# Where the lo half of a split weight begins in its buffer, in a one-core encoder kernel

## The chip, the core and the metric

The kernel runs on one core of a Trainium2 chip. The metric is the device time of one execution in microseconds; the time of before is the median of three executions.

## The reference, cut to what matters

A two-layer encoder over 256 tokens of width 1024, in float32. Each layer is a chain of matrix products with four mixers in between:

```python
for i in range(DEPTH):                     # 2
    h = rmsnorm(x, norm1_g[i])
    z = h @ w_in[i]
    ...
    gt = jax.nn.sigmoid(gates.reshape(B, S, N_BRANCH, D_MODEL))
    m = (gt[:, :, 0] * (ya @ proj_a[i]) + gt[:, :, 1] * (yb @ proj_b[i])
         + gt[:, :, 2] * (yc @ proj_c[i]) + gt[:, :, 3] * (yd @ proj_d[i]))
    x = x + m @ w_out[i]
    h2 = rmsnorm(x, norm2_g[i])
    x = x + jnp.square(jax.nn.relu(h2 @ mlp_w1[i])) @ mlp_w2[i]
```

## The kernel before, in words

**Splitting.** A float32 product is made of three matmuls of a shorter format (float32r). Each operand is split into a hi part (a rounded copy) and a lo part (what the rounding lost). `mm3` (L246) issues hi by hi, hi by lo and lo by hi, on the lines L248, L249 and L250, all adding to one accumulator.

**Weights.** The weights come from memory in units of up to 1 MB, in the fixed order of `layer_order` (L90). SP issues their DMAs ahead into three raw buffers (`load_raw`, L205). `split_to` (L217) cuts a unit into two halves and makes two tiles of each: ScalarE copies the raw half into the hi tile (L230), VectorE subtracts hi from raw into the lo tile (L231). There are five hi buffers and five lo buffers of 1152 columns; a half has up to 1024 columns, or 1152 in one unit. `take` (L236) hands the halves out in order and keeps up to four split ahead.

**Where a half begins.** `part_offsets` (L85) gives the column at which the hi and the lo half begin in their buffers. Units in MOVING begin at column 112 (448 bytes) in both, all others at column 0. In the program's layout every hi and lo buffer starts 128 bytes past a multiple of 512, every activation tile (pools `s4` and `s2`) 64 bytes past one, and the constant `gm` 192 bytes past one. So a half of a MOVING unit begins 64 past a multiple of 512, as the activations do, and any other half 128 past. Slices of 128 columns are 512 bytes, so all slices of a half have the residue of its start.

**Two ways of use.** `chunk_tm` (L252) and the down projection of the MLP load the activations into the array (128 tokens) and stream the weights over them, 288 to 512 columns at a time: these are the MOVING units, in the profile `w<-hi,act`, `w<-lo,act` and `acc<-...`. `unit_fm` (L285) does the reverse: 128 columns of the weights are loaded into the array, and the activations of 256 tokens stream. In the profile these are `w<-act,hi` and `w<-act,lo` (what streams stands first, then what is loaded): the gates (16 units a layer), the four output projections (8), the MLP's up projection (14 of its 16 units) and the query, key and convolution inputs (8).

In `unit_fm` all k steps of a block run back to back, three matmuls each:

```python
for k in range(nk):
    self.mm3(p[:, b % 2, :], wh[:, k, c], wl[:, k, c], ah[:, k, :], al[:, k, :], k == 0, k == nk - 1)
```

So L248 loads hi and streams the activations' hi part, L249 loads the same hi slice again and streams their lo part, and L250 loads the lo slice and streams the hi part. A triple is one k step. The chip loads the weights of a matmul while the one ahead of it streams (PEld in the profile).

Other work that the prediction names: L695 multiplies the constant `gm` with a split operand `g`; the dilated mixer's units use `chunk_tm` with a stride of 2, so that every second token is loaded.

Of the kernel before, what the change touches and what calls it, by code (L numbers as in the profile page):

```python
# [81 lines left out]
MOVING = {u for u, (mat, k0, nk, cols, off, n) in PLAN.items() if n // nk > 256 and not u.startswith("proj")}  # L82


def part_offsets(l, u):  # L85

    return (112, 112) if u in MOVING else (0, 0)


def layer_order():  # L90
# [38 lines left out]
class Kern:  # L129
# [87 lines left out]
    def split_to(self, upto):  # L217
        nc = self.nc
        while self.hi_ < min(upto, len(self.halves)):
            i, j = self.halves[self.hi_]  # L220
            self.load_raw(i + 1)
            hs = halves(self.units[i][1])
            (k0, k1), (c0, c1) = hs[j]
            src = self.raw[i][:, k0:k1, c0:c1]
            if j == len(hs) - 1:
                del self.raw[i]
            nk, w = k1 - k0, c1 - c0
            hi, lo = [self.hp.tile([128, 1152], F32, tag=t, name=self.nm(t))[:, o:o + nk * w].rearrange(
                "p (k c) -> p k c", k=nk) for t, o in zip(("hi", "lo"), part_offsets(*self.units[i]))]
            nc.scalar.copy(hi.bitcast(F32R), src)  # L230
            nc.vector.tensor_sub(lo.bitcast(F32R), src, hi)  # L231
            self.ready[self.hi_] = (hi.bitcast(F32R), lo.bitcast(F32R))
            self.hi_ += 1
            self.load_raw(i + NRAW)
# [1090 lines left out]
```

## Time and profile before

| | |
|---|---|
| median of 3 executions | 1109.08 us (1108.99 to 1109.64) |
| the profiled execution | 1108.95 us |
| its span, first to last instruction | 1107.1 us |
| granted TensorE clock over the span | 1.000 |
| PE busy | 1089.1 us, 98% |
| weight loads (PEld) busy | 979.8 us, 89% |
| VectorE busy | 729.4 us, 66% |
| ScalarE busy | 581.8 us, 53% |
| moved by DMA | 195.84 MB, mean 177 GB/s |

The span is the time from the program's first to its last instruction in the one profiled execution; what lies around it makes the rest of that execution's time. Matmuls are pipelined: a matmul's reported duration overlaps the next one's, so the distance between two starts tells what a matmul costs in a stream, and the duration tells it only in comparison with others of the same form.

### The profile page before, as it was taken

What the parts mean: (1) busy time and instruction counts of PE and PEld (TensorE: products, weight loads), DVE (VectorE), ACT (ScalarE), POOL (GpSimd) and SP (SyncE); (2) the same over time, 40 slices, a digit from 0 to 9 for tenths busy, and PEclk for the clock granted to TensorE, in tenths of its full rate; (3) what the DMA queues carried; (4) which work ended last, traced back from release to release, by engine and by line L of the source; (5) the groups of instructions that cost most, each with busy time, mean ns of one, the idle gap of its engine ahead of it and who ended that gap; (6) DMA issues with size and microseconds to landing.
All of it is one profiled execution on the core that took longest, in us unless ns stands there. A gap on an engine that the chain in (4) does not pass through costs nothing.

```text
span 1107.1 us, 17951 instructions
## 1 busy us (share of the span) xinstructions
PE 1089.1 (98%) x7374; PEld 979.8 (89%) x7374; DVE 729.4 (66%) x1053; ACT 581.8 (53%) x902; POOL 65.3 (6%) x72
## 2 busy tenths in 40 slices
PE   7999999999999999999999999999999999999998
PEld 4889778999999789889879997889999998999997
DVE  5787777656766668655565777776587667555554
ACT  6765555555544565454547554555464456544442
POOL 1001132000100000000000013130001000000000
PEclk9999999999999999999999999999999999999999
DMA  8443544755354555545445434548443655454542
GB/s 306 167 154 123 188 166 152 213 168 191 115 218 163 199 204 188 190 154 227 155 150 210 156 135 185 185 138 213 164 163 136 226 191 186 156 214 167 209 172 77
DMA packets 41527, 195.84 MB, mean 177 GB/s; under 512 B 5025, under 2 KB 16194, under 8 KB 20196
## 3 DMA queue, kind: packets, MB, share of 16 engines
q1 hardware_dynamic: 41444, 194.68, 49.7%
q8 instruction: 58, 0.95, 0.3%
q14 instruction: 25, 0.20, 0.0%
HBM read 193.58 MB, written 1.08 MB: 176 GB/s over the span
## 4 chain that ended last, share of the span: by engine, by line
PE 91%; DVE 4%; POOL 2%; issue 1%; ACT 1%; DMA 0%; SPq 0%; DVEq 0%; POOLq 0%; ACTq 0%
PE w L248 22%; PE w L250 22%; PE w L249 22%; PE acc L248 5%; PE acc L249 5%; PE acc L250 5%; PE tp L317 3%; DVE lo L231 2%; POOL s L310 2%; PE p L824 1%; PE p L854 1%; PE p L1028 1%; PE p L948 1%; PE p L913 1%; PE w L614 1%
## 5 line engine op out<-in xcount | busy, mean ns | idle before, releaser
L231 DVE TENSOR_TENSOR lo<-raw,hi 128x1024 fp32r<-128x1024 f32 (+2 forms) x352 | 414.5, 1198 | 136.8 <-ACT hi L230 132.9
L248 PE MATMUL w<-act,hi 128*128 128x256 f32 x1440 | 409.6, 284 | 0.0
L250 PE MATMUL w<-act,lo 128*128 128x256 f32 x1440 | 402.7, 280 | 0.0
L249 PE MATMUL w<-act,hi 128*128 128x256 f32 x1440 | 402.7, 280 | 0.0
L230 ACT CAST hi<-raw 128x1024 fp32r<-128x1024 f32 (+2 forms) x352 | 348.9, 1031 | 27.6 <-ACT hi L230 13.0
L248 PEld LDWEIGHTS w<-act,hi 128*128 128x128 f32 x1440 | 271.9, 189 | 8.9 <-issue 3.7
L249 PEld LDWEIGHTS w<-act,hi 128*128 128x128 f32 x1440 | 272.4, 189 | 2.0 <-issue 0.7
L250 PEld LDWEIGHTS w<-act,lo 128*128 128x128 f32 x1440 | 271.0, 188 | 0.0
L248 PE MATMUL w<-hi,act 128*128 128x512 f32 (+1 forms) x416 | 164.9, 396 | 1.6 <-ACT act L404 1.3
L250 PE MATMUL w<-hi,act 128*128 128x512 f32 (+1 forms) x416 | 160.2, 385 | 1.4 <-DVE act L325 1.4
L249 PE MATMUL w<-lo,act 128*128 128x512 f32 (+1 forms) x416 | 160.0, 385 | 1.4 <-DVE lo L231 1.4
L248 PEld LDWEIGHTS w<-hi,act 128*128 128x128 f32 x416 | 79.2, 190 | 17.7 <-issue 1.7
L250 PEld LDWEIGHTS w<-hi,act 128*128 128x128 f32 x416 | 79.1, 190 | 17.7 <-DVE act L325 2.3
L249 PEld LDWEIGHTS w<-lo,act 128*128 128x128 f32 x416 | 79.2, 191 | 16.8 <-DVE lo L231 2.3
L248 PE MATMUL acc<-hi,u 128*128 128x512 f32 x224 | 87.6, 391 | 0.0
L249 PE MATMUL acc<-lo,u 128*128 128x512 f32 x224 | 87.4, 390 | 0.0
L250 PE MATMUL acc<-hi,u 128*128 128x512 f32 x224 | 87.1, 389 | 0.0
L1109 ACT ACTIVATE u<-w 128x512 f32<-128x512 f32 x28 | 16.7, 598 | 115.6 <-PE w L250 115.6
L1111 DVE TENSOR_TENSOR u<-u 128x512 f32<-128x512 f32 x28 | 19.4, 692 | 87.6 <-ACT u L1109 87.5
L1060 ACT ACTIVATE sg<-w 128x512 f32<-128x512 f32 x32 | 19.1, 597 | 86.9 <-PE w L250 86.9
L310 POOL TENSOR_TENSOR s<-s,mhalf 128x8 f32<-128x8 f32 (+2 forms) x32 | 55.2, 1726 | 2.7
L250 PEld LDWEIGHTS acc<-hi,u 128*128 128x128 f32 x224 | 42.1, 188 | 9.0
(231 smaller groups left out, 977.7 us busy)
## 6 DMA issues: line engine op xcount, KB each, us to landing
raw<-in_w SPq DMA_DIRECT2D x166, 1024.0 KB, 4.9
raw<-in_w SPq DMA_DIRECT2D x8, 512.0 KB, 3.3
raw<-in_w SPq DMA_DIRECT2D x4, 576.0 KB, 4.3
b<-bias SPq DMA_DIRECT2D x32, 64.0 KB, 6.7
b<-bias SPq DMA_DIRECT2D x16, 128.0 KB, 6.8
b<-bias SPq DMA_DIRECT2D x8, 256.0 KB, 5.3
w<-in_hw SPq DMA_DIRECT2D x2, 512.0 KB, 6.5
decay<-in_decay SPq DMA_DIRECT2D x2, 512.0 KB, 7.1
```

The costliest lines, as they stand in the source:

```text
L230: nc.scalar.copy(hi.bitcast(F32R), src)
L231: nc.vector.tensor_sub(lo.bitcast(F32R), src, hi)
L248: mm(out, lhsT=lh, rhs=rh, start=start, stop=False)
L249: mm(out, lhsT=lh, rhs=rl, start=False, stop=False)
L250: mm(out, lhsT=ll, rhs=rh, start=False, stop=stop)
L310: self.nc.gpsimd.tensor_tensor(y, x, self.mhalf[:, 0:n], ALU.pow)
L317: self.nc.tensor.transpose(p[:, i, :], s, self.ident)
L614: nc.tensor.matmul(ps[e], lhsT=fw[:, e, ri], rhs=src[:, e], start=True, stop=True)
L824: nc.tensor.matmul(ps[par][:, c0:c0 + k.stop - k.start], lhsT=st.q[g][r, hp, c], rhs=kk, start=True, stop=True)
L1060: self.unit_fm(f"gate_{b}.{2 * i + j}", act, lambda _, ps: nc.scalar.activation(sg[:, 2 * j:2 * j + 2], ps, AF.Tanh, scale=0.5))
L1109: nc.scalar.activation(r, ps, AF.Relu)
L1111: nc.vector.tensor_mul(sq, r, r)
```

## The change

In units that are not in MOVING the lo half begins at column 32 of its buffer, 128 bytes further on than before. The hi half stays at column 0.

```diff
 def part_offsets(l, u):
 
-    return (112, 112) if u in MOVING else (0, 0)
+    return (112, 112) if u in MOVING else (0, 32)
```

The loaded lo slices thus begin 256 bytes past a multiple of 512, where the hi slices begin 128 past and the streamed activations 64 past one. No instruction is added or taken away.

## Rows read from the trace of the kernel before

**Rows 1.** The page, parts 1 and 2: busy time and share; granted clock in 40 slices.

```profile
PE 1089.1 (98%) x7374; PEld 979.8 (89%) x7374; DVE 729.4 (66%) x1053; ACT 581.8 (53%) x902; POOL 65.3 (6%) x72
...
PEclk9999999999999999999999999999999999999999
```

**Rows 2.** The page, part 4: chain that ended last, shares of the span by engine.

```profile
PE 91%; DVE 4%; POOL 2%; issue 1%; ACT 1%; DMA 0%; SPq 0%; DVEq 0%; POOLq 0%; ACTq 0%
```

**Rows 3.** The page, part 5: groups by line and operation, whole run (busy us, mean ns).

```profile
L248 PE MATMUL w<-act,hi 128*128 128x256 f32 x1440 | 409.6, 284 | 0.0
L250 PE MATMUL w<-act,lo 128*128 128x256 f32 x1440 | 402.7, 280 | 0.0
L249 PE MATMUL w<-act,hi 128*128 128x256 f32 x1440 | 402.7, 280 | 0.0
L248 PEld LDWEIGHTS w<-act,hi 128*128 128x128 f32 x1440 | 271.9, 189 | 8.9 <-issue 3.7
L249 PEld LDWEIGHTS w<-act,hi 128*128 128x128 f32 x1440 | 272.4, 189 | 2.0 <-issue 0.7
L250 PEld LDWEIGHTS w<-act,lo 128*128 128x128 f32 x1440 | 271.0, 188 | 0.0
```

**Rows 4.** Groups by form in the stretch 103.5 to 108.6 us.

```profile
L249 PE MATMUL w<-act,hi 128*128 128x256 f32 x16 | 4.4, 276 | 0.0
...
L249 PEld LDWEIGHTS w<-act,hi 128*128 128x128 f32 x16 | 3.0, 188 | 0.0
```

**Rows 5.** Groups by form in the stretch 857.5 to 862.8 us.

```profile
L249 PE MATMUL w<-act,hi 128*128 128x256 f32 x16 | 4.5, 281 | 0.0
...
L250 PEld LDWEIGHTS w<-act,lo 128*128 128x128 f32 x16 | 3.0, 188 | 0.0
...
L248 PEld LDWEIGHTS w<-act,hi 128*128 128x128 f32 x15 | 2.9, 192 | 0.0
```

**Rows 6.** Timeline of PE, 103.4 to 108.9 us: start us, us; first and last.

```profile
103.36 0.28 PE L248 MATMUL w<-act,hi 128*128 128x256 f32 x1
...
108.69 0.28 PE L250 MATMUL w<-act,lo 128*128 128x256 f32 x1
```

**Rows 7.** Timeline of PE, 857.4 to 863.1 us: first and last.

```profile
857.37 0.28 PE L248 MATMUL w<-act,hi 128*128 128x256 f32 x1
...
863.02 0.28 PE L248 MATMUL w<-act,hi 128*128 128x256 f32 x1
```

**Rows 8.** Groups by form from 915 us to the end.

```profile
L249 PEld LDWEIGHTS w<-act,hi 128*128 128x128 f32 x224 | 42.9, 192 | 0.5
```

**Rows 9.** Groups by form in the stretch 253.6 to 258.9 us.

```profile
L250 PEld LDWEIGHTS w<-act,lo 128*128 128x128 f32 x15 | 2.9, 192 | 0.0
```

**Rows 10.** The page, part 5: the down projection's matmuls and loads.

```profile
L248 PE MATMUL acc<-hi,u 128*128 128x512 f32 x224 | 87.6, 391 | 0.0
...
L250 PEld LDWEIGHTS acc<-hi,u 128*128 128x128 f32 x224 | 42.1, 188 | 9.0
```

**Rows 11.** Groups by form, 114.4 to 119.4 us: activations loaded with every second column.

```profile
L249 PE MATMUL w<-lo,act 128*128 128x512 f32 x8 | 3.2, 396 | 0.0
...
L249 PEld LDWEIGHTS w<-lo,act 128*128 128x128 f32 x7 | 1.4, 196 | 0.3
```

**Rows 12.** Timeline of PE, 63.7 to 64.45 us.

```profile
63.83 0.64 PE L695 MATMUL p<-gm,g 128*128 128x256 f32 x4
64.31 0.28 PE L248 MATMUL w<-act,hi 128*128 128x256 f32 x1
```

**Rows 13.** VectorE's splits (rows 11's stretch, rows 5's), busy share, PE's waits on it.

```profile
L231 DVE TENSOR_TENSOR lo<-raw,hi 128x1024 fp32r<-128x1024 f32 x4 | 4.7, 1218 | 0.0
...
L231 DVE TENSOR_TENSOR lo<-raw,hi 128x1024 fp32r<-128x1024 f32 x1 | 1.2, 1227 | 0.3 <-ACT hi L230 0.3
...
PE w L249 <- DVE lo L231: 1.4, 2, 1.0
```

## The prediction

> **What bounds the kernel now.** I read four views in this order: the page's busy times, its chain, its costliest groups, and then the same groups in short stretches. TensorE is busy for 98% of the span and its granted clock is at full speed (the upper level, 2.4 GHz) from the first slice to the last [rows 1]. The chain of work that ended last runs through PE for 91% of its length; VectorE stands in it with 4%, DMA with 0% [rows 2]. So a nanosecond taken from or added to a matmul is, to a tenth or so, a nanosecond of the end.
>
> The change touches weights that are loaded into the array. Those are the `w<-act` matmuls of 256 columns: 1440 triples of the lines L248, L249, L250, 409.6 + 402.7 + 402.7 us of busy PE [rows 3]. In a triple L248 and L249 both load the hi part, and L250 loads the lo part. Each load runs beside the matmul ahead of it, so the load for L250 runs while L249 streams the lo activations.
>
> These triples have two speeds, with the same instructions and shapes. In one stretch every matmul is reported with 276 ns and every load with 188 ns [rows 4]; in another every matmul has 281 ns, and of the three loads one has 192 ns and two have 188 [rows 5]. What counts is the distance from start to start. In the quick stretch 47 steps take 108.69 - 103.36 = 5.33 us, 113.4 ns each [rows 6]; in the slow one 48 steps take 863.02 - 857.37 = 5.65 us, 117.7 ns each [rows 7]. That is 4.3 ns a matmul and 13 ns a triple, at an unchanged clock.
>
> How many triples are slow? The L249 and L250 groups have 402.7 us / 1440 = 279.65 ns on average [rows 3]; between 276 and 281 that is 73%. So about 1050 triples are slow and 390 quick. In the last stage, the second MLP, all 224 are slow: there L249's loads have 192 ns as their mean over the whole stage [rows 8]; in the stretch of rows 5 it is L248's; a stretch in which it is L250's, the lo load, exists too [rows 9]. So which load is long is not fixed by line: a stretch keeps the pattern that it entered with.
>
> **Are the loads and the streamed operand at odds over addresses?** In the program's layout the hi and lo buffers start 128 bytes past a multiple of 512 and the activations 64 bytes past one, so every load of a triple lies 64 bytes ahead of what streams. Three other spacings occur. The `acc` matmuls stream weights shifted by 448 bytes: load and stream start on the same residue, the loads take 188 ns and 512 columns are reported with 391 ns [rows 10]. Where the activations are loaded with every second column, so that the load passes over 1024 bytes, the load takes 196 ns and 512 columns have 396 ns [rows 11]. And L695, whose loads lie 128 bytes behind its stream, needs (64.31 - 63.83) / 4 = 120 ns for 256 columns [rows 12], more than the slow pattern. So spacing goes with time, a few ns a matmul, in either direction. What 192 bytes ahead costs, no row shows.
>
> The Trainium skill says otherwise ("SBUF — State Buffer", section "Who interferes with whom"): PE has two independent read ports, one for the moving operand and one for the weight load, and never waits on anyone; by that rule the change is worth 0 us. The trace does not bear the rule out as it stands: loads of one shape take 188 or 192 ns, with the matmuls beside them.
>
> **The change part by part.**
> 1. The lo buffer of the units that are not in MOVING is used from column 32 on. Its 1152 columns hold 32 + 1024, so it fits, and no instruction, wait or DMA is added or moved. The hi buffers, the activations and all MOVING units stay.
> 2. The split's subtraction (L231) writes 128 bytes further on. VectorE needs 1218 ns for a split of MOVING parts (the ones split in the stretch of rows 11), which land at another residue than their source, and 1227 ns for one whose source and target share a residue [rows 13]. I cost it at nothing, 9 ns either way at most; the 184 splits of that kind would make 1.7 us on VectorE, which is busy 66% [rows 1], and PE waits for these splits 1.4 us in the whole run [rows 13]. Were that cover gone, those 1.7 us would be the cost.
> 3. The L250 load lies 192 bytes ahead of its stream in place of 64. This is the term that decides. Gain at most: no slow triple is left, 1050 x 13 = 13.7 us. Loss: the 390 quick triples turn slow, 390 x 13 = 5.1 us; or every matmul costs what L695's does, 120 ns, so a triple costs 360 in place of 353 or 340: 1050 x 7 + 390 x 20 = 15 us.
>
> Between these ends I take half of the gain. The slow pattern needs one long load in each triple, and it is found on any of the three, which are alike in spacing. With one of three moved away, a stretch that would have its long load on L250 loses it, and a stretch that comes into a unit out of step has one place less at which to lock. Against taking the whole: the hi loads keep their place, and the group means (271.9, 272.4 and 271.0 us over 1440, or 188.8, 189.2 and 188.2 ns [rows 3]) say that the long load is more often on the hi loads of L248 and L249. So the sum: 0.5 x 13.7 = 6.8 us, less nothing for VectorE. The profiled execution took 1108.95 us (span 1107.1 and 1.85 around it), 0.13 under the median of 1109.08; 1108.95 - 6.8 = 1102.1, so 1102 us.
>
> **The rivals.**
> *The hi loads carry the pattern on (no change).* If the 192 ns load of L248 or L249 is what holds a stretch in step, the lo load's place doesn't matter; rows 5 and 8 speak for it, since the whole second MLP has its long load on L249. Only stretches of the kind of rows 9 would then be freed, and those may lock on a neighbour: 1109 us, within 2. The other way to no change is that the long load has nothing to do with residues, and that the two speeds are a matter of how a stretch begins. For it speaks that the quick and the slow stretches have the same spacing; against it rows 11 and 12. That is where the rule of two independent ports would lead: 1109 us. That the offset isn't applied I exclude, since the shift is in the one place where the buffers are cut.
>
> *The new place collides in the quick stretches too (slower).* It lies in the L250 load, and it decides where 192 bytes ahead is to the stream what 128 behind is in L695. Then the quick stretches lose their footing: 390 x 13 = 5.1 us, 1114 us; and up to 15 us, 1124 us, if each matmul of each triple reaches 120 ns. For it: L695's spacing is the nearest one of 128 bytes in the trace, and it is worse than 64. Against it: it was read on groups of four matmuls, which never settle.
>
> **How the numbers follow.** The forecast has 0.44: 73% of the triples are in slow stretches, so a disturbance has more of them to break than quick ones to spoil. Its own range goes from nearly all of the gain (1096) to a fifth of it (1106). No change has 0.24 (0.18 for the hi loads, 0.06 for a pattern that ignores residues), slower has 0.32. A measurement of this kernel can tell about 0.2%, 2.2 us, from no change, so the chances of faster, same and slower are those of the cases: 0.44, 0.24, 0.32. The likeliest time is 1102. The range goes from 1096, nearly the whole gain, over no change to 1115, just past the fall of all quick stretches; what lies outside, a whole gain or a doubled loss, is under 2 in 10.
>
> **What would show it.** Right: the L249 and L250 groups of `w<-act` come from a mean of 279.65 towards 278 or less, the stretch of the second MLP shows 276 where it had 281, the loads' means fall to 188, and nothing else changes by more than a microsecond. No change: the same means, and the 192 ns load still on L248 or L249 throughout. Slower: the stretch of rows 4 shows 281 or more, or two loads of a triple have over 190 ns. I would be wrong in the mechanism if the time moved while these means didn't: then VectorE's splits or the waits at the units' starts would have moved it.

## The result, and the profile after

The changed kernel takes 1097.72 us (median of 4 runs, 1097.32 to 1098.11), against 1109.1 us (1108.99 to 1109.64) for the kernel before on the same chip: a ratio of 0.9896 with a 95% interval of 0.9879 to 0.9914, so 11.4 us or 1.0% less. The profiled execution took 1098.07 us, with a span of 1096.3 us.

The page of the changed kernel, parts 1, 4 and 5 (busy us and share; the chain by engine; groups with busy us and mean ns), against [rows 1, 2, 3, 10]:

```profile
PE 1078.0 (98%) x7374; PEld 968.3 (88%) x7374; DVE 728.7 (66%) x1053; ACT 582.0 (53%) x902; POOL 65.2 (6%) x72
...
PEclk9999999999999999999999999999999999999999
...
PE 91%; DVE 4%; POOL 2%; issue 1%; DMA 1%; ACT 0%; SPq 0%; DVEq 0%; POOLq 0%; ACTq 0%
...
L248 PE MATMUL w<-act,hi 128*128 128x256 f32 x1440 | 405.3, 281 | 0.0
L250 PE MATMUL w<-act,lo 128*128 128x256 f32 x1440 | 398.4, 277 | 0.0
L249 PE MATMUL w<-act,hi 128*128 128x256 f32 x1440 | 398.2, 277 | 0.0
...
L248 PEld LDWEIGHTS w<-act,hi 128*128 128x128 f32 x1440 | 270.3, 188 | 8.9 <-issue 3.7
L249 PEld LDWEIGHTS w<-act,hi 128*128 128x128 f32 x1440 | 270.5, 188 | 2.0 <-issue 0.7
L250 PEld LDWEIGHTS w<-act,lo 128*128 128x128 f32 x1440 | 270.4, 188 | 0.0
...
L248 PE MATMUL acc<-hi,u 128*128 128x512 f32 x224 | 87.6, 391 | 0.0
```

PE is busy 11.1 us less, at the same share of the span and of the chain (98% and 91%) and the same clock. The `acc` group has not moved by 0.1 us; each `w<-act` group has lost 4.3 to 4.5 us. These three losses add up to 13.1 us, more than the time gained, because reported durations of pipelined matmuls overlap. Summing over the trace the distance from each `w<-act` start to the next start on PE gives 513.4 us before and 502.0 us after, 11.4 us less. The same sum for the matmuls that stream weights goes from 292.0 to 292.8, and for `acc` it stays at 174.8. So the whole gain is in the matmuls whose weights the change moved. The span is 1107.1 - 1096.3 = 10.8 us shorter.

The groups by form in the second MLP, from 905 us to the end, where nearly every triple was slow before [rows 8] (by the starts 216 of 223; seven that follow one another were quick), and then, from 915 us to the end, one of them before:

```profile
L248 PE MATMUL w<-act,hi 128*128 128x256 f32 x224 | 62.0, 277 | 0.0
L250 PE MATMUL w<-act,lo 128*128 128x256 f32 x224 | 61.9, 277 | 0.0
L249 PE MATMUL w<-act,hi 128*128 128x256 f32 x224 | 61.9, 276 | 0.0
L249 PEld LDWEIGHTS w<-act,hi 128*128 128x128 f32 x224 | 42.1, 188 | 0.5
```

```profile
L249 PE MATMUL w<-act,hi 128*128 128x256 f32 x224 | 62.9, 281 | 0.0
```

The load of L249 had 192 ns on average in this stage and now has 188; the matmuls had 281 and, with 276 to 277, are down to what the quick stretch showed [rows 4].

What is left of the slow pattern is its beginning. The timeline of PE in one unit of the first MLP, 494 to 500 us (start us, us); shown are starts of L248, one per triple:

```profile
494.13 0.28 PE L248 MATMUL w<-act,hi 128*128 128x256 f32 x1
...
494.49 0.28 PE L248 MATMUL w<-act,hi 128*128 128x256 f32 x1
...
494.84 0.28 PE L248 MATMUL w<-act,hi 128*128 128x256 f32 x1
...
495.18 0.28 PE L248 MATMUL w<-act,hi 128*128 128x256 f32 x1
...
499.26 0.28 PE L248 MATMUL w<-act,hi 128*128 128x256 f32 x1
```

The first triple takes 0.36 us, the second 0.35, and from the third on it is (499.26 - 494.84) / 13 = 0.340 us, 113.3 ns a matmul, as in [rows 6]. Before, a stretch could stay at 353 ns a triple to its end [rows 7]. Over the whole trace, counting from L248's start to the next matmul's wherever that follows within 0.4 us (1349 triples), 1217 triples take 343 ns or less after the change, and 348 did before. Against 340 ns each, the 1349 lose 1.9 us in all, where they lost 13.2.

VectorE did not pay: the 336 splits of 1024 columns took 403.4 us before and, in the groups by form after, 403.2. PE's waits on the splits came to 2.1 us in place of 1.4 [rows 13].

```profile
L231 DVE TENSOR_TENSOR lo<-raw,hi 128x1024 fp32r<-128x1024 f32 x336 | 403.2, 1221 | 128.0 <-ACT hi L230 123.6 <-PE w L250 0.2
...
PE w L249 <- DVE lo L231: 2.1, 3, 0.9
```

### The profile page after: what moved, and what is told of

It is laid out like the page before. It is cut to its first block, busy times and chain, and to the rows that moved or that the text cites. A ratio compares the mean times of both kernels' runs of the same rounds, so it can differ in the third digit from the quotient of the medians.

```text
span 1096.3 us, 17951 instructions
## 1 busy us (share of the span) xinstructions
PE 1078.0 (98%) x7374; PEld 968.3 (88%) x7374; DVE 728.7 (66%) x1053; ACT 582.0 (53%) x902; POOL 65.2 (6%) x72
## 4 chain that ended last, share of the span: by engine, by line
PE 91%; DVE 4%; POOL 2%; issue 1%; DMA 1%; ACT 0%; SPq 0%; DVEq 0%; POOLq 0%; ACTq 0%
PE w L248 22%; PE w L250 21%; PE w L249 21%; PE acc L248 5%; PE acc L249 5%; PE acc L250 5%; PE tp L317 3%; DVE lo L231 2%; POOL s L310 2%; DMA raw<-in_w 1%; PE p L824 1%; PE p L854 1%; PE p L1028 1%; PE p L948 1%; PE p L913 1%
## 5 line engine op out<-in xcount | busy, mean ns | idle before, releaser
L248 PE MATMUL w<-act,hi 128*128 128x256 f32 x1440 | 405.3, 281 | 0.0
L250 PE MATMUL w<-act,lo 128*128 128x256 f32 x1440 | 398.4, 277 | 0.0
L249 PE MATMUL w<-act,hi 128*128 128x256 f32 x1440 | 398.2, 277 | 0.0
L248 PEld LDWEIGHTS w<-act,hi 128*128 128x128 f32 x1440 | 270.3, 188 | 8.9 <-issue 3.7
L249 PEld LDWEIGHTS w<-act,hi 128*128 128x128 f32 x1440 | 270.5, 188 | 2.0 <-issue 0.7
L248 PE MATMUL w<-hi,act 128*128 128x512 f32 (+1 forms) x416 | 164.8, 396 | 1.4 <-ACT act L404 1.1
L249 PE MATMUL w<-lo,act 128*128 128x512 f32 (+1 forms) x416 | 160.1, 385 | 2.1 <-DVE lo L231 2.1
L249 PEld LDWEIGHTS w<-lo,act 128*128 128x128 f32 x416 | 79.2, 190 | 17.6 <-DVE lo L231 3.1
L248 PEld LDWEIGHTS w<-hi,act 128*128 128x128 f32 x416 | 79.1, 190 | 17.6 <-issue 1.7
L248 PE MATMUL acc<-hi,u 128*128 128x512 f32 x224 | 87.6, 391 | 0.0
L249 PE MATMUL acc<-lo,u 128*128 128x512 f32 x224 | 87.4, 390 | 0.0
```

The lines of the kernel that those rows point to most:

```text
L248: mm(out, lhsT=lh, rhs=rh, start=start, stop=False)
L249: mm(out, lhsT=lh, rhs=rl, start=False, stop=False)
L250: mm(out, lhsT=ll, rhs=rh, start=False, stop=stop)
```

## The experiments

Nearly every experiment sets the two offsets of the units that are not in MOVING, the second pair in `part_offsets`, and nothing else; one float is 4 bytes. Activations lie 64 bytes past a multiple of 512, hi and lo buffers 128. Shifts below are in bytes, hi first; the kernel before is (0, 0), the changed one (0, 128). All ratios are to the kernel before. Triples are counted as above, 1349 in every trace, and called quick at 343 ns or less.

**1. Both halves 128 bytes on: (128, 128).** If unlike places of hi and lo are what helps, moving hi as well must take the gain away.

```diff
-    return (112, 112) if u in MOVING else (0, 32)
+    return (112, 112) if u in MOVING else (32, 32)
```

> Both halves of a loaded weight begin at column 32, so all three loads of a triple lie 192 bytes ahead of what streams. Theory A (unlike spacing): the slow pattern needs three loads of one spacing, and the changed kernel is quick because its lo load differs; here they are alike again, so the slow stretches come back: 1104 to 1112 us, L249 and L250 groups at 279 to 281 ns. Theory B (residue): 192 bytes ahead is simply a better place than 64, load by load; here all three have it: 1094 to 1098 us, means of 276 to 277 ns.

Measured: 1112.56 us (1112.17 to 1114.31), ratio 1.0031 [1.0019, 1.0043]. Its page, and the PE timeline of one unit of 48 matmuls (first and last start):

```profile
L250 PE MATMUL w<-act,lo 128*128 128x256 f32 x1440 | 402.0, 279 | 0.0
L249 PE MATMUL w<-act,hi 128*128 128x256 f32 x1440 | 401.6, 279 | 0.0
L248 PEld LDWEIGHTS w<-act,hi 128*128 128x128 f32 x1440 | 270.0, 187 | 8.9 <-issue 3.7
L249 PEld LDWEIGHTS w<-act,hi 128*128 128x128 f32 x1440 | 270.3, 188 | 2.0 <-issue 0.7
L250 PEld LDWEIGHTS w<-act,lo 128*128 128x128 f32 x1440 | 270.3, 188 | 0.0
```

```profile
490.93 0.28 PE L248 MATMUL w<-act,hi 128*128 128x256 f32 x1
...
496.46 0.28 PE L250 MATMUL w<-act,lo 128*128 128x256 f32 x1
```

The gain is gone, as the theory of unlike places had it: 47 steps in 5.53 us are 117.7 ns each, the slow speed to the digit [rows 7]. That the place of the lo load is good by itself, whatever hi does, falls. Only 97 of the triples are quick. The loads tell something else: hardly any is long here (187 to 188 ns in every group; 33 of 4320 take 192), and the triples are slow all the same. So the 192 ns load, by which the prediction recognised a slow triple, is not what makes it slow.

**2. The hi half alone: (128, 0).** The two halves again lie 128 bytes apart, the other way round.

```diff
-    return (112, 112) if u in MOVING else (0, 32)
+    return (112, 112) if u in MOVING else (32, 0)
```

> The hi half begins at column 32 and the lo half at column 0: two loads of a triple lie 192 bytes ahead, one 64. Theory A (unlike spacing): as quick as the changed kernel, 1096 to 1100 us. Theory B (residue): two good loads in place of one, so no slower than the changed kernel and up to 2 us quicker, 1095 to 1098 us; if in B only the lo load's own place counts, it is back at 64 and the time at 1107 to 1110 us.

Measured: 1108.31 us (1107.85 to 1108.59), 0.9989 [0.9979, 0.9999]: a tenth of the gain. The groups by form of the stretch 100 to 110 us, and then those of the last 192 us:

```profile
L249 PE MATMUL w<-act,hi 128*128 128x256 f32 x24 | 6.8, 283 | 0.0
L248 PE MATMUL w<-act,hi 128*128 128x256 f32 x24 | 6.8, 283 | 0.0
L250 PE MATMUL w<-act,lo 128*128 128x256 f32 x24 | 6.7, 279 | 0.0
```

```profile
L248 PE MATMUL w<-act,hi 128*128 128x256 f32 x224 | 62.0, 277 | 0.0
L249 PE MATMUL w<-act,hi 128*128 128x256 f32 x224 | 61.9, 276 | 0.0
L250 PE MATMUL w<-act,lo 128*128 128x256 f32 x224 | 61.9, 276 | 0.0
```

The second MLP is as quick as with the change, and in the other stretch L248 and L249 are slower than in the slow stretch of before, 283 against 281 ns [rows 5]: by the starts its triples take 353 and 360 ns in turn. In the whole trace 588 triples are quick, more than the 348 of before, but most of the others alternate like this and cost more. Quick and slow stretches persist side by side at these places too; unlike spacing alone does not remove the slow one. That falls as the explanation.

**3. The lo half 512 bytes on: (0, 512).** The control for distance as such.

```diff
-    return (112, 112) if u in MOVING else (0, 32)
+    return (112, 112) if u in MOVING else (0, 128)
```

> The lo half begins 512 bytes further on, the hi half as before the change. If places count modulo 512 bytes (both theories), nothing changes: 1108 to 1110 us, means of 279.5 ns. Rival C: the change helped because the lo half no longer begins where its buffer begins, or lies further from the hi half, whatever the residue: 1096 to 1100 us.

Measured: 1109.24 us (1108.96 to 1109.79), 0.9996 [0.9987, 1.0005], and the six `w<-act` groups of its page are those of [rows 3] within 0.1 us. Distance as such does nothing; what counts is the place within a round.

**4. The lo half 64 bytes on: (0, 64).**

```diff
-    return (112, 112) if u in MOVING else (0, 32)
+    return (112, 112) if u in MOVING else (0, 16)
```

> The lo half begins 64 bytes further on, so its load lies 128 bytes ahead of the stream, the hi loads 64. Theory A (unlike spacing): any difference breaks the pattern, 1096 to 1100 us. Theory B (residue): the cost has a place of its own for each spacing; 128 ahead lies between 64 (slow for 73% of the triples) and 192 (quick), so 1098 to 1107 us.

Measured: 1116.44 us (1116.3 to 1118.16), 1.0067 [1.0052, 1.0082], slower than before. The unit of 48 matmuls in its timeline:

```profile
490.65 0.28 PE L248 MATMUL w<-act,hi 128*128 128x256 f32 x1
...
496.22 0.28 PE L250 MATMUL w<-act,lo 128*128 128x256 f32 x1
```

That is 5.57 / 47 = 118.5 ns a step, and in the whole trace no triple is quick. By the starts the long stretches go round in cycles of five triples, of 355, 354, 357, 348 and 359 ns. Neither theory had this: unlike halves can be worse than like ones. The prediction's slower rival comes true here, at another place than the one the change chose.

**5 and 6. The lo activations moved in place of the weights, and the control.** The weights lie as before. If what counts is the load against what streams beside it (the lo weights load while the lo activations stream), moving the lo activations instead should do the same. Those of the layers' normed activations, which 1216 of the 1440 triples stream, got a pool of four buffers, 448 bytes past a multiple of 512; in the control the same pool lies 64 past (the edit below without the `pad` tile, and with `PAD = 0`).

```diff
-        self.sm = P("sm", 42)
+        self.sm = P("sm", 40)
+        self.gap = P("gap", 1)
+        self.sl = P("sl", 4)
+        self.gap.tile([128, PAD], F32, name="pad")
...
-        self.hpair = self.acts(8)
+        self.hpair = [[self.t4([128, 4, 256], "act") for _ in range(2)],
+                      [self.sl.tile([128, 4, 256], F32, tag="sl", name=self.nm("act")) for _ in range(2)]]
...
-NS4, NS2, NRAW, NHL, LA = 23, 13, 3, 5, 4
+NS4, NS2, NRAW, NHL, LA = 19, 13, 3, 5, 4
+PAD = 96
```

> The weights as before the change; the lo halves of the layers' normed activations (what L249 streams in the gates, the MLP's up projection and the inputs; 1216 of 1440 triples) lie in buffers of their own at 448 past a multiple of 512 in place of 64. The lo load beside that stream is thus 192 bytes ahead of it, as in the changed kernel, and the hi loads beside the other two streams are 64 ahead. Theory D (each load against the stream beside it, in the order of the triple): the w<-act groups come to 276 to 278 ns as after the change, and the time lies 8 to 12 us under that of the kernel with the same buffers at residue 64. Theory E (the lo load against the hi loads, whatever streams): the groups stay at 279 to 281 ns and the two times agree within 3 us, but for the chunk matmuls that load these buffers.

> The same buffers of their own for the lo activations, at the old residue of 64: both theories expect the kernel before, 1107 to 1112 us and means of 279 to 281 ns; more only if the four buffers taken from the other pool make work wait.

Measured: 1114.08 us (1113.97 to 1114.54), 1.0045 [1.0028, 1.0062], with the pool moved; 1109.55 (1108.46 to 1110.15), 1.000 [0.999, 1.0009], in the control, so the new pool by itself costs nothing. Moved activations (`mm3` stands three lines lower in this kernel):

```profile
L251 PE MATMUL w<-act,hi 128*128 128x256 f32 x1440 | 410.4, 285 | 0.0
L252 PE MATMUL w<-act,hi 128*128 128x256 f32 x1440 | 404.3, 281 | 0.0
L253 PE MATMUL w<-act,lo 128*128 128x256 f32 x1440 | 403.1, 280 | 0.0
```

The stream's place counts too, since 4.5 us lie between two kernels that differ in this pool's place alone, and 4.2 of them are between the `w<-act` starts (517.7 against 513.5 us); the matmuls that stream weights, some of which load from the pool, differ by 0.3 (292.9 against 292.6). But it went the wrong way for the theory of one load against the stream beside it, which falls. Neither theory had a time so far over the control's.

**7. Both halves where the activations are: (448, 448).**

```diff
-    return (112, 112) if u in MOVING else (0, 32)
+    return (112, 112) if u in MOVING else (112, 112)
```

> Both halves begin at column 112, so every load begins on the residue of what streams beside it, as in the down projection. If the two halves need unlike places (what e1 left standing), a slow pattern stays: 1107 to 1114 us. If spacing 0 is free of trouble whatever the length of the stream (the down projection's loads have 188 ns), 1095 to 1099 us.

Measured: 1122.38 us (1122.18 to 1124.69), 1.0123 [1.0108, 1.0138], the slowest of all. Its page and the timeline of one unit of 48:

```profile
L250 PE MATMUL w<-act,lo 128*128 128x256 f32 x1440 | 407.4, 283 | 0.0
L249 PE MATMUL w<-act,hi 128*128 128x256 f32 x1440 | 407.3, 283 | 0.0
L248 PEld LDWEIGHTS w<-act,hi 128*128 128x128 f32 x1440 | 275.8, 192 | 8.9 <-issue 3.7
L249 PEld LDWEIGHTS w<-act,hi 128*128 128x128 f32 x1440 | 275.9, 192 | 2.0 <-issue 0.7
L250 PEld LDWEIGHTS w<-act,lo 128*128 128x128 f32 x1440 | 275.7, 191 | 0.0
```

```profile
493.00 0.28 PE L248 MATMUL w<-act,hi 128*128 128x256 f32 x1
...
498.63 0.28 PE L250 MATMUL w<-act,lo 128*128 128x256 f32 x1
```

5.63 / 47 = 119.8 ns a step: the 120 ns that L695 showed [rows 12], now in a long settled stream and at another spacing. Load and stream start on the same residue, as in the `acc` matmuls [rows 10], but with 256 columns streaming nearly every load is long (3788 of 4320 take 192 ns) and nearly every matmul late. Both expected ranges, which end at 1114 us, are missed.

**8 and 11. The lo half alone there: (0, 448) and (0, 192).**

```diff
-    return (112, 112) if u in MOVING else (0, 32)
+    return (112, 112) if u in MOVING else (0, 112)
```

```diff
-    return (112, 112) if u in MOVING else (0, 32)
+    return (112, 112) if u in MOVING else (0, 48)
```

> Only the lo half moves, to column 112: its load lies level with the stream (spacing 0), the hi loads 64 ahead, so the lo load is 64 bytes behind the hi loads in place of 128 ahead. Theory D and E both allow any outcome from 1096 to 1117 us; if what counts is only the distance between lo and hi, 64 either way, it is as slow as the shift by 64 bytes, 1114 to 1118 us; if a lo load that comes earlier in the round of 512 bytes is what helps, 1096 to 1100 us.

> Hi as before the change, lo 192 bytes past it: its load lies 256 bytes ahead, the far side of the round of 512. If quick places for lo form one region around 192 ahead, 1096 to 1102 us. If 192 is a single place between costly ones (as 128 ahead was, 1116 us), 1104 to 1118 us.

Measured: 1114.46 us (1114.38 to 1114.78), 1.0047 [1.0032, 1.0062], and 1114.7 us (1114.45 to 1115.14), 1.0049 [1.0034, 1.0064]. The six `w<-act` groups of the two pages are the same to the last digit, these three among them:

```profile
L248 PE MATMUL w<-act,hi 128*128 128x256 f32 x1440 | 411.5, 286 | 0.0
L249 PE MATMUL w<-act,hi 128*128 128x256 f32 x1440 | 405.4, 282 | 0.0
L250 PE MATMUL w<-act,lo 128*128 128x256 f32 x1440 | 404.7, 281 | 0.0
```

No triple is quick in either; nearly all take 353 ns. The time of (0, 448) lies in the range expected if only the 64 bytes between hi and lo counted, but the pattern isn't that of (0, 64) with its cycle of five.

**9. Both moved, 128 bytes apart: (64, 192).** The halves stand to each other as in the changed kernel, but 64 bytes further on against the activations.

```diff
-    return (112, 112) if u in MOVING else (0, 32)
+    return (112, 112) if u in MOVING else (16, 48)
```

> The pair of the changed kernel, both moved on by 64 bytes: the lo half still begins 128 bytes past the hi half, but hi loads lie 128 ahead of the streams and lo loads 256. Theory E (the distance from hi to lo decides): as the changed kernel, 1096 to 1100 us, w<-act means of 276 to 277 ns. Theory G (the pair's place against the activations decides too): not quick, 1104 to 1120 us, means of 279 to 283 ns.

Measured: 1116.78 us (1116.63 to 1118.8), 1.0072 [1.0057, 1.0087], 19 us over the changed kernel, whose distance from hi to lo it shares. So that distance alone is not the cause either; where the pair lies belongs to it. Whether that means its place against the activations or its place in the round by itself, this run doesn't tell, since the activations stay where they are.

**10. (384, 0)**, to see whether the swapped pair of experiment 2 comes back 256 bytes further, **and 12. (0, 256)**, the same for the kernel before.

```diff
-    return (112, 112) if u in MOVING else (0, 32)
+    return (112, 112) if u in MOVING else (96, 0)
```

```diff
-    return (112, 112) if u in MOVING else (0, 32)
+    return (112, 112) if u in MOVING else (0, 64)
```

> The distance of 128 bytes from hi to lo (modulo 512) a second time, at another place: the hi half begins at column 96, so hi loads lie 64 behind the streams, and lo loads 64 ahead. Theory E: 1096 to 1100 us. Theory G: anything else, from the levels seen so far (no load, two loads or three loads of a triple with 6.7 ns each) 1104 to 1123 us.

> Hi as before the change, lo 256 bytes past it: its load lies 320 bytes ahead. If the quick region reaches the far half of the round, 1096 to 1102 us; if two loads of a triple stay costly, as in most of the places tried, 1106 to 1117 us.

Measured: 1107.9 us (1107.36 to 1108.59), 0.9988 [0.9978, 0.9997], which is experiment 2 again; and 1109.29 us (1108.95 to 1109.78), 0.9999 [0.999, 1.0009]. The page of (0, 256):

```profile
L248 PE MATMUL w<-act,hi 128*128 128x256 f32 x1440 | 409.7, 284 | 0.0
L249 PE MATMUL w<-act,hi 128*128 128x256 f32 x1440 | 402.7, 280 | 0.0
L249 PEld LDWEIGHTS w<-act,hi 128*128 128x128 f32 x1440 | 272.4, 189 | 2.0 <-issue 0.7
```

This is [rows 3] again. With experiments 3, 8 and 11 that makes two places of the lo half and one of the hi half, each with its like 256 bytes on: the round is 256 bytes, not 512.

**All of them, modulo 256:**

| hi, lo shift | us | triples |
|---|---|---|
| 0, 128 (the change) | 1097.7 | quick, after up to four late ones at the start |
| 128, 0 | 1108 | 44% quick, most others 353 and 360 ns in turn |
| 0, 0 (before) | 1109 | some 73% slow (353 ns), the others quick |
| 128, 128 | 1112.6 | 353 ns, hardly a load long; 7% quick |
| 0, 192 | 1114.5 | 353 ns, none quick |
| 0, 64 | 1116.4 | cycles of five, none quick |
| 64, 192 | 1116.8 | cycles of four (365, 352, 355, 348 ns), none quick |
| 192, 192 | 1122.4 | 360 ns, nearly all loads long; none quick |

No version beats the changed kernel. The experiments show that the places of both loads and of the stream set the speed of a triple, and that the weights' places count modulo 256 bytes. They count together: moving lo alone gains 11.4 us and moving hi alone 1, so if each half had a cost of its own, moving both would give some 1097 us; it gave 1112.6. Why this pair of places is the quick one stays open. So does the question whether places count against the activations or in the round by themselves. Moving all activations and weights by the same amount would separate these; it wasn't tried, nor were steps of 32 bytes and another order of the three matmuls.

## Why the prediction came out

**The bound held.** PE was and is 98% busy and 91% of the chain, and of the 11.4 us that its `w<-act` starts gained the span has 10.8.

**Steps 1 and 2, the offset and the splits at nothing: right.** The splits changed by 0.2 us in 403, and PE's waits for them grew by 0.7 us.

**Step 3, the lo load's new place: right in sign, its size off.** The term was 13.7 us at most, of which the prediction took half, 6.8. It measured 11.4, five sixths. The ceiling was good, since it came from starts in the timeline and from the group's mean: by the starts the triples lost 13.2 us before, and of the 1.9 us that they still lose 1.7 are at the beginnings. (That all 224 triples of the second MLP were slow was read from a rounded mean of the loads; seven were quick.) What failed is the half. It was argued from the group means, by which the hi loads carried the 192 ns more often and would keep most slow stretches. Of the 994 loads with 192 ns before, 847 were indeed hi loads, but though these stayed in place, 53 of them are left. Experiment 1 shows besides that, at other places, a slow triple needs no long load, so the share of the long loads was no measure of what would stay. After the change the slow pattern doesn't hold in any long stretch.

**The reason given beside it was too wide.** "One place less at which to lock" would have held for any unlike place. (0, 64), (0, 192) and (128, 0) move one half too, and the first two are 5 to 7 us slower than before. The forecast named the mechanism, a pattern held by places, but nothing in the trace of before could tell this place from the bad ones. Of the three places of the lo half within the round that were tried besides its old one, this one alone gains: that the time fell was in part luck.

**The rival of no change falls.** The hi loads kept their place and carried the pattern on in no long stretch; in the second MLP L249's load came down from 192 to 188 ns. Its other form, that places don't matter, falls more plainly: experiment 7 and the changed kernel issue the same instructions and lie 1122.38 - 1097.72 = 24.7 us apart. By the rule of the Trainium skill ("SBUF — State Buffer", section "Who interferes with whom") that PE has independent read ports for its streams and its loads and never waits on anyone, the two would take the same time. The traces don't agree, with 113.3 against 119.8 ns a matmul; what it is inside PE or its reads that takes longer, they don't show.

**The slower rival had its numbers right and its place wrong.** Its 1114 to 1124 us hold what four other places gave: 1114.5, 1116.4, 1116.8 and 1122.4. It even reached the 120 ns of L695 in experiment 7. Its chance of 0.32 was not too much for a place that no row showed.

**The readings by spacing were partly false.** Rows 10 were read as a sign that load and stream on one residue get on well; with 256 columns that is the worst case of all. And the spacings were counted modulo 512, where the chip showed 256: 192 bytes ahead is the same as 64 behind.

## What to carry to other kernels

Where TensorE is the bound and a group of equal matmuls shows two speeds at one clock, compare distances between starts in a quick and a slow stretch: their difference times the slow count is a ceiling for what the layout can give, and here five sixths of it came. Try several offsets of the loaded weights within one round (256 bytes here) rather than argue for one, because neighbours 64 bytes apart lay on both sides of the kernel before. Move no buffer of such a kernel for other reasons without timing it: one pool of four buffers shifted cost 4.5 us in experiment 5 with the work unchanged.

## What the runs showed of the hardware that was not expected

- The places of the loaded weights count modulo 256 bytes: (0, 0) = (0, 256) = (0, 512) within 0.2 us, (0, 192) = (0, 448) within 0.3 us, (128, 0) = (384, 0) within 0.5 us.
- A settled stretch repeats a pattern to the nanosecond or nearly so. It can be one triple long, with 340 ns, 353 (3 x 117.7) or 360 (3 x 119.8); two triples, 353 and 360, with (128, 0); four, 365, 352, 355 and 348, with (64, 192); or five, 355, 354, 357, 348 and 359, with (0, 64).
- A long load and a late matmul are two things: with (128, 128) the triples are slow with loads of 187 to 188 ns, with (192, 192) the groups of loads have 191 to 192.
- The pattern has a memory. In the kernel before, and with (128, 0), quick and slow stretches of the same places exist side by side, each lasting; with (0, 128) no stretch begins with more than four late triples, and they pass into the quick pattern by themselves. Addresses above the 256 bytes don't pick the speed: in the program's layout of the kernel before, seven triples from 205.91 us on and seven from 279.51 us on load and stream from the same addresses to the byte, and six of them take 2.04 us in the one stretch and 2.12 in the other (timeline of PE, starts of L248; 340 and 353 ns a triple). That leaves how a stretch begins, as the second form of the prediction's first rival had it; no run tests this by itself. The places decide whether a slow pattern can last.

```profile
205.91 0.28 PE L248 MATMUL w<-act,hi 128*128 128x256 f32 x1
...
207.95 0.28 PE L248 MATMUL w<-act,hi 128*128 128x256 f32 x1
...
279.51 0.28 PE L248 MATMUL w<-act,hi 128*128 128x256 f32 x1
...
281.63 0.28 PE L248 MATMUL w<-act,hi 128*128 128x256 f32 x1
```
